# Turning tiles by way of DRAM instead of block by block, HGRN keys on TensorE, and a longer rest between narrow visits

## The chip, the core and the metric

The kernel runs on one core of a Trainium2 chip. The metric is the device time of one execution in microseconds (us). Engines are named as in the profile: PE is TensorE (matmuls; PEld is its weight load), DVE is VectorE, ACT is ScalarE, POOL is GpSimd, and SP is SyncE, whose queue issues nearly all DMAs.

## What is computed

One layer of a hybrid encoder on a sequence of 512 frames with 2048 features, in float32. One input projection feeds 16 RWKV-7 heads of 64 channels and 8 HGRN2 heads of 128 channels. Their gated outputs are concatenated, projected back, added to the input and normalized:

```python
proj = einsum('btd,dc->btc', x, w_in)
rw, hg = token_shift(proj[..., :RWKV_COLS]), proj[..., RWKV_COLS:]
# RWKV-7, per head: state S (64 x 64), one step a frame
S = S * w_t + (S @ -kk_t) (kk_t * a_t)^T + v_t k_t^T ;  o_t = S @ r_t
o = group_norm(o) * gn_w + gn_b + sum(r * k * r_k) * v ;  o_rwkv = o * silu(z)
# HGRN2, per head: gated linear recurrence, evaluated in chunks
o = chunkwise(silu(q), log_f, k, i) ;  o_hgrn = rms_norm(o) * g_norm_w * silu(z)
y = layer_norm(ALPHA * x + concat(o_rwkv, o_hgrn) @ w_out)
```

## The kernel before

The two projections are the bulk of the work. A float32 product is made from three float32r matmuls (high by high, high by low, low by high), so both operands are split into a high and a low part, on ScalarE and VectorE. Weights come in tiles `wr` of 512 KB, of which two are in flight; the split parts are `wh` and `wl`. These matmuls, issued at line 457, are called "main". The sequence `_order()` fixes which columns of the input projection are made when: eight RWKV pairs (two heads of 64 to a tile of 128 channels) and eight HGRN heads, in four groups of two pairs and two heads. The output projection follows, in four column blocks of 512; it takes its 16 k-tiles in the order `korder`, with pairs and heads 6 and 7 last.

Everything else (the recurrences, gates and norms) is put between the main matmuls by a planner, `Plan`, which runs while the program is written. It keeps a clock for each engine and SP, the time when each tile will be ready, and the time when it will be free, all from written-out costs. Side work lies in queues of Python generators. A generator yields operations, or tests that must hold before it goes on (`room(...)`: buffers are free; `has(...)`: another generator has delivered; `landed(...)`: PE would find the tiles ready by the planner's clock). After each main matmul `pump()` takes what can go next from every queue. The order that comes out is fixed in the program; on the chip the engines wait for each other by semaphores.

PE work has three modes: `main`, `whole` (128 x 128 stationary, float32) and `narrow` (a part of the array: 64 x 128, 128 x 32, 32 x 32 and so on). `Plan.worth` lets no narrow operation start in another mode until `REST` has gone by since the last narrow one ended (`self.rest = end + self.REST`, line 132).

The parts that the change touches:

- `send` (line 308) issues a DMA on SP's queue and moves the planner's SP clock.
- `turned` (line 397) transposes a tile without PE: VectorE transposes every 32 x 32 block in place (`dtr`), and DMAs from SBUF to SBUF then move each block to its place, one DMA for each block row and block column: 16 for `bk` and for the keys of a head, 8 for v.
- `rwkv_prep` (line 628) turns `bk` (beta and k, 128 x 1024) and v, the latter into the lower half of `z`, tile name `zz`, 128 x 8 x 128. `from_v` (751), `outputs` (772) and `rwkv_scan` (836) use `z` as the moving operand, chunk by chunk of 64 frames.
- `rwkv_finish` (901) ends a pair: group norm, four transposes on PE (line 925) into a PSUM tile, and scale, bias, `bv` and gate on VectorE.
- `hgrn_out` (1061) ends a head. It turns three blocks of keys, by `turned` for heads 0 to 5 and on PE for heads 6 and 7 (line 1075); makes the states and the output; norms it; and turns the output with four transposes on PE (line 1109).
- `put_gated` writes the gated tiles of pairs 0 to 5 and heads 0 to 5 to DRAM (`spill`); they are read back for the output projection.

Of the kernel before, what the change touches and what calls it, by code (L numbers as in the profile page):

```python
# [15 lines left out]
P = 128  # L16
# [7 lines left out]
NCH = T // C  # L24
# [38 lines left out]
class Plan:  # L63
# [178 lines left out]
def mixer_kernel(ctx, tc, head, x_r, w_all, par, up, ln_wb, consts, hmask, out):  # L242
# [41 lines left out]
    def drop(*tiles):  # L284
        for t in tiles:
            name = t.tensor.name
            plan.slots[tags.pop(name)].append((plan.used.get(name, plan.count), plan.busy[name][0]))

    def room(**need):

        return lambda: all(plan.free(tag, n) for tag, n in need.items())
# [13 lines left out]

        return test

    def send(o, i, cost=0.44):

        nc.sync.dma_start(o, i)  # L310
        plan.clock["sp"] = max(plan.clock["sp"], plan.clock["pe"]) + cost


    def size(ap):
# [55 lines left out]
    def dtr(o, i):  # L370
        return dve_op([i], o, lambda: dve.transpose(o, i), per=0.0019)
# [208 lines left out]
    def chunks(t):  # L580
        return t.rearrange("p (c s) -> p c s", s=C)
# [42 lines left out]
            ups.append(upw)  # L624

    hc = [slice(64 * h, 64 * h + 64) for h in range(2)]

    def rwkv_prep(S, p):
        if p == 0:
# [111 lines left out]
        S["bv"] = r  # L741

        yield room(zz=1)
        z = take("zz", [P, NCH, P])
        yield room(ksq=1)
        tmp = take("ksq")
        yield from turned(z, chunks(v), chunks(tmp), rows=2, base=64)
        drop(v, tmp)
        S["zz"] = z

    def from_v(SS, sc):

        yield lambda: all("zz" in S for S in SS)
        zs = [S["zz"] for S in SS]
        yield room(main=2, mix=1)
        yield landed(*zs, sc)
        pss = [take("main") for _ in SS]
        for half, (z, ps) in enumerate(zip(zs, pss)):
            for c in range(NCH):
                for h in range(2):  # L760
                    yield mm(ps[hc[h], c * C : c * C + C], sc[64:128, 0, half * 16 + 2 * c + h],
                             z[64:128, c, hc[h]])

        def keep():
            for z, ps in zip(zs, pss):
                for h in range(2):
                    yield copy(z[0:64, :, hc[h]], chunks(ps[hc[h]]))
                drop(ps)

        return keep  # L770

    def outputs(SS, sc):

        yield room(mix=2)
        pss = [take("mix") for _ in SS]
        for half, (S, po) in enumerate(zip(SS, pss)):
            z = S["zz"]
            yield lambda z=z: by_now(z)
            for c in range(0, NCH, 2):
                for h in range(2):  # L780
                    for e in range(2):
                        yield mm(po[hc[e], c // 2 * P + 64 * h : c // 2 * P + 64 * h + 64],
                                 sc[:, 1, half * 16 + 2 * (c + e) + h], z[:, c + e, hc[h]])
# [52 lines left out]
    def rwkv_scan(SS, sc):  # L836

        pcs, ars, bks, zzs, os = ([S[n] for S in SS] for n in ("pc", "ar", "bk", "zz", "o"))
        yield room(bd=4, rt=2)
        bdss = [[take("bd", [P, P]) for _ in range(2)] for _ in SS]
        rts = [take("rt", [P, P]) for _ in SS]

        def block(ps, h):
            return ps[hc[h], h * 64 : h * 64 + 64]

        for rt, bds, o in zip(rts, bdss, os):
            yield memset(rt[64:128], 0.0)  # L850
            for t in bds:
                yield memset(t, 0.0)
            yield memset(o[0:64, 0], 0.0)
        olds = [None] * 2
        for c in range(NCH):
            more = c < NCH - 1
            zs = [zz[:, c] for zz in zzs]
            news = [bds[c % 2] for bds in bdss]
            pxs = []
            if c > 0:  # L860
                yield landed(*olds)
                yield room(mix=2)
                for ar, old in zip(ars, olds):
                    pxs.append(take("mix"))
                    yield mm(pxs[-1][:, :P], ar[:, c], old)
                for rt, px, z in zip(rts, pxs, zs):
                    yield stt(rt[0:64], px[0:64, :P], -1.0, z[0:64], ALU.mult, ALU.subtract)
                if more:
                    for new, old, pc in zip(news, olds, pcs):
                        yield act(new, old, AF.Copy, scale=pc[:, c : c + 1])  # L870
            else:
                for rt, z in zip(rts, zs):
                    yield copy(rt[0:64], z[0:64], scale=-1.0)
            yield landed(*rts)
            yield room(mix=2)
            psas = [take("mix") for _ in SS]
            for half, (psa, rt) in enumerate(zip(psas, rts)):
                i = half * 16 + 2 * c
                yield mm(psa[:, :P], sc[:, 0, i : i + 2].rearrange("p h t -> p (h t)"), rt)
            for psa, z in zip(psas, zs):  # L880
                for h in range(2):
                    yield copy(z[0:64, hc[h]], block(psa, h))
                drop(psa)
            for px, o in zip(pxs, os):
                yield copy(o[64 * (c % 2) : 64 * (c % 2) + 64, c // 2], px[64:128, :P])
                drop(px)
            if more:
                yield landed(*zzs)
                yield room(mix=2)
                pds = [take("mix") for _ in SS]  # L890
                for pd, bk, z in zip(pds, bks, zs):
                    yield mm(pd[:, :P], bk[:, c], z)
                for pd, new, pc in zip(pds, news, pcs):
                    for h in range(2):
                        yield stt(new[hc[h], hc[h]], block(pd, h), pc[hc[h], c : c + 1],
                                  new[hc[h], hc[h]], ALU.mult, ALU.add)
                    drop(pd)
                olds = news
        drop(*ars, *bks, *pcs, *rts, *bdss[0], *bdss[1])

    def rwkv_finish(S, p):
# [16 lines left out]
        yield room(g=1, ksq=1)  # L918
        g = take("g")
        sz = take("ksq")  # L920
        z = S["z"]
        yield landed(o_all)
        po = take("mix")
        for j in range(4):
            yield tr(po[:, j * P : j * P + P], o_all[:, j])
        yield act(sz, z, AF.Tanh, scale=0.5)
        yield stt(g, po, hcol(HGW, p), S["bv"], ALU.mult, ALU.add)
        drop(po)
# [132 lines left out]
    def hgrn_out(S, h, q, k, dt_, dg, tot, tots):  # L1061
# [1 line left out]
        yield room(g=1)  # L1063
        g = take("g")
        kt, state = tiles(g)[:, 0:3], tiles(k)[:, 0:3]
        if h < 6:
            yield room(ksq=1)
            tmp = take("ksq")
            yield from turned(kt, tiles(k)[:, 0:3], tiles(tmp)[:, 0:3])
            drop(tmp)  # L1070
        else:
            yield landed(k)
            ps = take("mix")
            for t in range(3):
                yield tr(ps[:, t * P : t * P + P], k[:, t * P : t * P + P])
            yield copy(kt, tiles(ps)[:, 0:3])
            drop(ps)
        yield has(S, "i")
        yield room(rs=1)
        i_all = S["i"]  # L1080
# [25 lines left out]
        yield landed(o2)  # L1106
        pn = take("mix")
        for j in range(4):
            yield tr(pn[:, j * P : j * P + P], o2[:, j * P : j * P + P])
        yield has(S, "g")  # L1110
        yield stt(g, pn, hcol(HHW, h), S["g"], ALU.mult, ALU.mult)
        drop(S["g"], pn, o2)
        put_gated(8 + h, g)

    def silu2(ps, put):
# [561 lines left out]
```

## Time and profile before

| | |
|---|---|
| median of three runs | 1049.99 us (1049.23 to 1050.55) |
| the profiled execution | 1049.55 us |
| its span, first to last instruction | 1047.8 us |
| PE busy | 1039.1 us (99%), 7324 matmul records |
| DVE, ACT, POOL busy | 756.7, 437.9, 39.0 us |
| granted TensorE clock | 1.000 |
| DMA, main queue | 97824 packets, 114.57 MB |

In the profile, a row of the groups reads: line, engine, operation, output tile <- input tiles, shape, count | total busy time, mean of one in ns | idle time of the engine before them and what ended it. Buffer numbers are left out of tile names, so `q<-q` is any tile of the `q4` buffers from any other. A timeline row reads: start and duration in us, engine, line, operation, shape, count. A waits row reads: who <- for whom: total us, times, longest. The line of a helper stands for all who call it: 329 is every float32 matmul (`mm`), 333 every transpose on PE (`tr`), 310 every DMA (`send`), 371 every transpose on VectorE (`dtr`).

### The profile page before, as it was taken

Reading aid. Unit: us, or ns where it says so; the run is one execution under the profiler, and the core shown is the slowest. Engines: PE = TensorE matmul, PEld = TensorE weight load, DVE = VectorE, ACT = ScalarE, POOL = GpSimd, SP = SyncE. Lnnn points to the kernel's source line nnn. Section 1 sums busy time; section 2 is a strip of 40 time slices with the busy share of each in tenths; the row PEclk is TensorE's granted clock in tenths of the full one; section 3 lists DMA queues with packets and bytes.
Section 4 is the critical chain, followed back from the end, with each engine's and each line's share of the span. In section 5 each row is a group of like instructions: output and inputs, shape, how many; then the busy total and the mean of one; then the engine's idle time right before and its main releaser. Section 6 shows DMA issues by size and latency. Waiting matters only on the chain.

```text
span 1047.8 us, 18965 instructions
## 1 busy us (share of the span) xinstructions
PE 1039.1 (99%) x7324; PEld 864.3 (82%) x7324; DVE 756.7 (72%) x1649; ACT 437.9 (42%) x871; POOL 39.0 (4%) x81
## 2 busy tenths in 40 slices
PE   9999999999999999999999999999999999999997
PEld 8888888888888888887888888888888888888885
DVE  7474898767768987578689866686898878625556
ACT  6444433545344345353443354534434454223321
POOL 0000000000100000001000000010000001000000
PEclk9999999999999999999999999999999999999999
DMA  8135343222253532233534222225243244445613
GB/s 333 51 104 124 96 105 102 65 90 79 84 134 94 127 102 66 70 96 89 137 92 124 82 70 80 84 82 134 83 129 88 72 161 173 140 131 159 204 60 131
DMA packets 98058, 115.98 MB, mean 111 GB/s; under 512 B 67120, under 2 KB 68912, under 8 KB 97840
## 3 DMA queue, kind: packets, MB, share of 16 engines
q1 hardware_dynamic: 97824, 114.57, 37.5%
q8 instruction: 58, 0.95, 0.4%
q14 instruction: 32, 0.26, 0.1%
q10 hardware_dynamic: 144, 0.20, 0.1%
HBM read 99.92 MB, written 7.34 MB: 102 GB/s over the span
## 4 chain that ended last, share of the span: by engine, by line
PE 98%; DVE 1%; DMA 0%; issue 0%; SPq 0%; DVEq 0%
PE main L457 74%; PE mix L329 11%; PE mix L457 8%; PE main L1202 3%; PE main L329 2%; PE mix L333 1%; PE mix L1152 0%; DMA g<-ksq 0%; DVE inv L361 0%; DVE inv L352 0%; SPq L310 0%; DVE zz L394 0%; DVE stats L1559 0%; DVEq L1673 0%; DVE t L394 0%
## 5 line engine op out<-in xcount | busy, mean ns | idle before, releaser
L457 PE MATMUL main<-xh,wl 128*128 128x512 f32 x864 | 341.8, 396 | 0.0
L457 PE MATMUL main<-xh,wh 128*128 128x512 f32 x864 | 341.0, 395 | 0.0
L457 PE MATMUL main<-xl,wh 128*128 128x512 f32 x864 | 340.2, 394 | 0.0
L342 ACT ACTIVATE wh<-wr 128x512 fp32r<-128x512 f32 x299 | 187.0, 627 | 245.5 <-PE main L457 187.0
L352 DVE TENSOR_TENSOR wl<-wr,wh 128x512 fp32r<-128x512 f32 x299 | 203.2, 681 | 65.4 <-ACT wh L342 64.0
L457 PEld LDWEIGHTS main<-xl,wh 128*128 128x128 f32 x864 | 162.4, 188 | 33.2
L457 PEld LDWEIGHTS main<-xh,wh 128*128 128x128 f32 x864 | 162.5, 188 | 32.5
L457 PEld LDWEIGHTS main<-xh,wl 128*128 128x128 f32 x864 | 162.4, 188 | 32.6
L457 PE MATMUL main<-wh,xh 128*128 128x512 f32 (+1 forms) x262 | 102.2, 390 | 0.0
L457 PE MATMUL main<-wl,xh 128*128 128x512 f32 (+1 forms) x262 | 102.1, 390 | 0.0
L457 PE MATMUL main<-wh,xl 128*128 128x512 f32 (+1 forms) x262 | 102.0, 389 | 0.0
L457 PEld LDWEIGHTS main<-wh,xl 128*128 128x128 f32 x262 | 49.2, 188 | 9.8
L457 PEld LDWEIGHTS main<-wh,xh 128*128 128x128 f32 x262 | 49.2, 188 | 9.9
L457 PEld LDWEIGHTS main<-wl,xh 128*128 128x128 f32 x262 | 49.3, 188 | 9.5
L343 ACT ACTIVATE t<-main,om 128x512 f32<-128x512 f32 x33 | 22.3, 687 | 50.8 <-PE main L457 40.8
L361 DVE SCALAR_TENSOR_TENSOR t<-main,pr,t 128x511 f32<-128x511 f32 x33 | 24.3, 745 | 23.8 <-ACT t L343 23.5
L352 DVE TENSOR_TENSOR inv<-inv,inv 64x30 f32<-64x30 f32 (+14 forms) x120 | 38.6, 321 | 2.7
L352 DVE TENSOR_TENSOR inv<-inv 64x30 f32<-64x30 f32 (+14 forms) x120 | 38.5, 321 | 2.7
L361 DVE SCALAR_TENSOR_TENSOR bd<-mix,pc,bd 64x64 f32<-64x64 f32 x112 | 31.7, 283 | 11.0 <-PE mix L329 8.8
L352 DVE TENSOR_TENSOR t<-t,tot 128x256 f32<-128x256 f32 x96 | 37.2, 416 | 1.6 <-PE mix L329 1.3
L343 ACT ACTIVATE t<-main 128x512 f32<-128x512 f32 x32 | 18.7, 596 | 46.5 <-PE main L457 46.5
L384 POOL TENSOR_TENSOR rs<-rs,mhalf 128x4 f32<-128x4 f32 x8 | 10.8, 1346 | 496.9 <-DVE rs L358 496.9
(223 smaller groups left out, 1328.6 us busy)
## 6 DMA issues: line engine op xcount, KB each, us to landing
wr<-w_all SPq DMA_DIRECT2D x156, 512.0 KB, 3.6
q<-head SPq DMA_DIRECT2D x15, 448.0 KB, 5.5
q<-q SPq DMA_DIRECT2D x128, 32.0 KB, 2.6
g<-x_r SPq DMA_DIRECT2D x16, 256.0 KB, 3.8
spill<-g SPq DMA_DIRECT2D x12, 256.0 KB, 3.9
out<-q SPq DMA_DIRECT2D x12, 256.0 KB, 2.4
t<-spill SPq DMA_DIRECT2D x10, 256.0 KB, 4.1
zz<-ksq SPq DMA_DIRECT2D x64, 32.0 KB, 3.1
```

The lines of the kernel that those rows point to most:

```text
L329: return Op([("pe", cost, lambda: pe.matmul(o, l, r, start=start, stop=stop, **kw))], [l, r], [o], mode="narrow" if narrow else "main" if ...
L333: return Op([("pe", 0.11, lambda: pe.transpose(o, i, ident))], [i], [o])
L342: return "act", cost, lambda: sc_e.activation(o, i, f, scale=scale)
L343: return "act", cost, lambda: sc_e.activation(o, i, f, scale=scale, bias=bias)
L352: return dve_op([a, b], o, lambda: dve.tensor_tensor(o, a, b, f), base=0.16 if o.shape[0] < P and size(o) == C and o.tensor.name in tags e ...
L361: return dve_op([a, b], o, lambda: dve.scalar_tensor_tensor(o, a, s, b, f1, f2), per=0.00113, base=0.085 if o.shape[0] == P else 0.25 if s ...
L384: lambda: pool.tensor_tensor(o, i, mhalf[:, : size(o)], ALU.pow))], [i], [o])
L457: pe.matmul(ps, l, r, start=first and i == 0, stop=last and i == 2)
L1202: pe.matmul(pss[a], *ops, start=k == 0 and low == of == 0, stop=k == KT - 1 and low == 1)
```

## The change

`REST` goes from 1.5 to 2.5 us. `turned` now goes through DRAM: VectorE transposes the 32 x 32 blocks, one DMA writes the tile to a DRAM tile `far`, and one DMA for each 32 rows (four, or two for v) reads it back in its turned order. All blocks of one row then lie together, so the layout of what comes back is blocks of 32 columns, chunk by chunk. `z` keeps that layout ([128, 4, 8, 32] instead of [128, 8, 128]) and its users index it so; `bk` is copied to the old layout once more, on ScalarE or VectorE. Pairs 0 to 5 and heads 0 to 5 turn their ends through `turned` instead of on PE. The keys of heads 0 to 5 are transposed on PE, as those of 6 and 7 were. `from_v`, `outputs` and `rwkv_scan` do the same matmuls and copies on the new layout; of them the diff shows one line each of two. Where it says `else:`, the four transposes and the product of before follow.

```diff
-    REST = 1.5
+    REST = 2.5
...
-    def turned(dst, src, tmp, rows=4, base=0):
-        name = dst.tensor.name
-        yield dtr(tmp, src)
+    def turned(dst, src, tmp, base=0):
+        c = src.shape[1]
+        n = src.shape[2] // 32
+        yield dtr(tmp, src.rearrange("p c (b f) -> p b c f", f=32))
         yield lambda: by_now(tmp)
-        for a in range(4):
-            for b in range(rows):
-                yield lambda: plan.clock["sp"] <= plan.clock["pe"] + 0.2
-                o = base + 32 * b
-                send(dst[o : o + 32, :, 32 * a : 32 * a + 32],
-                     tmp[32 * a : 32 * a + 32, :, 32 * b : 32 * b + 32], 0.65)
-        plan.ready[name] = plan.busy[tmp.tensor.name] = (plan.clock["sp"] + 2.6, "dma")
+        far = dpool.tile([4, 32, n, c * 32], F32, tag=nm("far"), name=nm("far"))
+        yield lambda: plan.clock["sp"] <= plan.clock["pe"]
+        send(far.rearrange("a p b r -> (a p) b r"), tmp.rearrange("p b c f -> p b (c f)"))
+        at = plan.clock["sp"] + 3.7
+        plan.busy[tmp.tensor.name] = (at, "dma")
+        yield lambda: plan.clock["pe"] >= at
+        for b in range(n):
+            yield lambda: plan.clock["sp"] <= plan.clock["pe"]
+            o = base + 32 * b
+            send(dst[o : o + 32].rearrange("p a c f -> p a (c f)"), far[:, :, b].rearrange("a p r -> p a r"))
+        plan.ready[dst.tensor.name] = plan.busy[dst.tensor.name] = (plan.clock["sp"] + 3.5, "dma")
...
@@ rwkv_prep
-        yield from turned(bk, bk, tmp)
-        drop(tmp)
+        flat = bk.rearrange("p c t -> p (c t)")
+        yield from turned(blocks(flat, NCH), bk, blocks(tmp.rearrange("p c t -> p (c t)"), NCH))
+        yield copy(tmp.rearrange("p c (a f) -> p a c f", f=32), blocks(flat, NCH))
+        drop(bk)
+        S["bk"] = tmp
...
-        z = take("zz", [P, NCH, P])
+        z = take("zz", [P, 4, NCH, 32])
...
-        yield from turned(z, chunks(v), chunks(tmp), rows=2, base=64)
+        yield from turned(z, chunks(v), blocks(tmp, NCH), base=64)
@@ from_v, rwkv_scan
-                             z[64:128, c, hc[h]])
+                             z[64:128, hb[h], c])
...
-            zs = [zz[:, c] for zz in zzs]
+            zs = [zz[:, :, c] for zz in zzs]
...
@@ rwkv_finish
+        if p < 6:
+            yield from turned(blocks(S["ot"], 4), o_all, blocks(g, 4))
...
+        if p < 6:
+            yield act(in_blocks(g), blocks(S["ot"], 4).rearrange("p a c f -> p c a f"), AF.Identity,
+                      scale=hcol(HGW, p), bias=hcol(HGB, p))
+            yield act(sz, z, AF.Tanh, scale=0.5)
+            yield tt(g, g, S["bv"], ALU.add)
+        else:
+...
         yield stt(z, sz, 1.0, z, ALU.add, ALU.mult)
-        yield stt(g, g, hcol(HGB, p), z, ALU.add, ALU.mult)
+        if p < 6:
+            yield tt(g, g, z)
+        else:
+            yield stt(g, g, hcol(HGB, p), z, ALU.add, ALU.mult)
...
@@ hgrn_out
-        if h < 6:
-            yield room(ksq=1)
-            tmp = take("ksq")
-            yield from turned(kt, tiles(k)[:, 0:3], tiles(tmp)[:, 0:3])
-            drop(tmp)
-        else:
+        yield landed(k)
+        ps = take("mix")
+        for t in range(3):
+            yield tr(ps[:, t * P : t * P + P], k[:, t * P : t * P + P])
+        yield copy(kt, tiles(ps)[:, 0:3])
...
+        if h < 6:
+            yield from turned(blocks(o2, 4), tiles(o2), blocks(g, 4))
+            yield has(S, "g")
+            yield act(in_blocks(g), blocks(o2, 4).rearrange("p a c f -> p c a f"), AF.Copy, scale=hcol(HHW, h))
+            yield tt(g, g, S["g"])
+            drop(S["g"], o2)
+        else:
+...
```

More of the change, by code (lines that the diff above doesn't have):

```diff
@@ L306, in landed, with send @@
         return test
-    def send(o, i, cost=0.44):
+    def send(o, i):
         nc.sync.dma_start(o, i)
-        plan.clock["sp"] = max(plan.clock["sp"], plan.clock["pe"]) + cost
+        plan.clock["sp"] = max(plan.clock["sp"], plan.clock["pe"]) + 0.44
     def size(ap):
@@ L395, in copy, with in_blocks, blocks @@
         return Op([act_way(o, i, AF.Copy, scale), ("dve", 0.075 + size(o) * 0.00105 + moved(o, i), f)], [i], [o])
-    def turned(dst, src, tmp, rows=4, base=0):
-        name = dst.tensor.name
-        yield dtr(tmp, src)
+    def turned(dst, src, tmp, base=0):
+        c = src.shape[1]
+        n = src.shape[2] // 32
+        yield dtr(tmp, src.rearrange("p c (b f) -> p b c f", f=32))
         yield lambda: by_now(tmp)
-        for a in range(4):
-            for b in range(rows):
-                yield lambda: plan.clock["sp"] <= plan.clock["pe"] + 0.2
-                o = base + 32 * b
-                send(dst[o : o + 32, :, 32 * a : 32 * a + 32],
-                     tmp[32 * a : 32 * a + 32, :, 32 * b : 32 * b + 32], 0.65)
-        plan.ready[name] = plan.busy[tmp.tensor.name] = (plan.clock["sp"] + 2.6, "dma")
+        far = dpool.tile([4, 32, n, c * 32], F32, tag=nm("far"), name=nm("far"))
[9 more added lines that the diff above has]
+        plan.ready[dst.tensor.name] = plan.busy[dst.tensor.name] = (plan.clock["sp"] + 3.5, "dma")
+    def in_blocks(t):
+        return t.rearrange("p (c a f) -> p c a f", a=4, f=32)
+    def blocks(t, c):
+        return t.rearrange("p (a c f) -> p a c f", c=c, f=32)
     splits = plan.queue()
@@ L626, in mixer_kernel @@
     hc = [slice(64 * h, 64 * h + 64) for h in range(2)]
+    hb = [slice(2 * h, 2 * h + 2) for h in range(2)]
     def rwkv_prep(S, p):
@@ L766, in keep @@
                 for h in range(2):
-                    yield copy(z[0:64, :, hc[h]], chunks(ps[hc[h]]))
+                    yield copy(z[0:64, hb[h]], ps[hc[h]].rearrange("p (c a f) -> p a c f", c=NCH, f=32))
                 drop(ps)
@@ L782, in outputs @@
                         yield mm(po[hc[e], c // 2 * P + 64 * h : c // 2 * P + 64 * h + 64],
-                                 sc[:, 1, half * 16 + 2 * (c + e) + h], z[:, c + e, hc[h]])
+                                 sc[:, 1, half * 16 + 2 * (c + e) + h], z[:, hb[h], c + e])
         for S, po in zip(SS, pss):
@@ L847, in block, with by32 @@
             return ps[hc[h], h * 64 : h * 64 + 64]
+        def by32(t):
+            return t.rearrange("p (a f) -> p a f", f=32)
         for rt, bds, o in zip(rts, bdss, os):
@@ L866, in rwkv_scan @@
                 for rt, px, z in zip(rts, pxs, zs):
-                    yield stt(rt[0:64], px[0:64, :P], -1.0, z[0:64], ALU.mult, ALU.subtract)
+                    yield stt(by32(rt[0:64]), by32(px[0:64, :P]), -1.0, z[0:64], ALU.mult, ALU.subtract)
                 if more:
@@ L872, in rwkv_scan @@
                 for rt, z in zip(rts, zs):
-                    yield copy(rt[0:64], z[0:64], scale=-1.0)
+                    yield copy(by32(rt[0:64]), z[0:64], scale=-1.0)
             yield landed(*rts)
@@ L881, in rwkv_scan @@
                 for h in range(2):
-                    yield copy(z[0:64, hc[h]], block(psa, h))
+                    yield copy(z[0:64, hb[h]], by32(block(psa, h)))
                 drop(psa)
@@ L917, in rwkv_finish @@
         yield has(S, "z", "bv")
-        yield room(g=1, ksq=1)
+        yield room(g=1)
         g = take("g")
+        if p < 6:
+            yield from turned(blocks(S["ot"], 4), o_all, blocks(g, 4))
+        yield room(ksq=1)
         sz = take("ksq")
         z = S["z"]
[L922 to L928, printed above, removed]
+        if p < 6:
[4 more added lines that the diff above has]
+        else:
+            yield landed(o_all)
+            po = take("mix")
+            for j in range(4):
+                yield tr(po[:, j * P : j * P + P], o_all[:, j])
+            yield act(sz, z, AF.Tanh, scale=0.5)
+            yield stt(g, po, hcol(HGW, p), S["bv"], ALU.mult, ALU.add)
+            drop(po)
         yield stt(z, sz, 1.0, z, ALU.add, ALU.mult)
-        yield stt(g, g, hcol(HGB, p), z, ALU.add, ALU.mult)
+        if p < 6:
+            yield tt(g, g, z)
+        else:
+            yield stt(g, g, hcol(HGB, p), z, ALU.add, ALU.mult)
         drop(z, S["bv"], S["ot"], sz)
@@ L1065, in hgrn_out @@
         kt, state = tiles(g)[:, 0:3], tiles(k)[:, 0:3]
-        if h < 6:
-            yield room(ksq=1)
-            tmp = take("ksq")
-            yield from turned(kt, tiles(k)[:, 0:3], tiles(tmp)[:, 0:3])
-            drop(tmp)
-        else:
[L1072 to L1077, printed above, removed]
+        yield landed(k)
[3 more added lines that the diff above has]
+        yield copy(kt, tiles(ps)[:, 0:3])
+        drop(ps)
         yield has(S, "i")
@@ L1105, in hgrn_out @@
         S["used"]()
[L1106 to L1112, printed above, removed]
+        if h < 6:
[5 more added lines that the diff above has]
+        else:
+            yield landed(o2)
+            pn = take("mix")
+            for j in range(4):
+                yield tr(pn[:, j * P : j * P + P], o2[:, j * P : j * P + P])
+            yield has(S, "g")
+            yield stt(g, pn, hcol(HHW, h), S["g"], ALU.mult, ALU.mult)
+            drop(S["g"], pn, o2)
         put_gated(8 + h, g)
```

## The prediction, made before the change was run

> **What bounds the kernel now.** I read the head of the page first, then the chain that ended last, then what TensorE waited for.
>
> ```profile
> span 1047.8 us, 18965 instructions
> PE 1039.1 (99%) x7324; PEld 864.3 (82%) x7324; DVE 756.7 (72%) x1649; ACT 437.9 (42%) x871; POOL 39.0 (4%) x81
> DVE  7474898767768987578689866686898878625556
> PE 98%; DVE 1%; DMA 0%; issue 0%; SPq 0%; DVEq 0%
> ```
>
> TensorE is 98% of the chain. VectorE comes second at 72%, with slices at 8 and 9 tenths, but holds 1% of the chain. So almost the whole time is the sum of what TensorE is given to do; work put on other engines costs nothing until TensorE has to wait for it. These are two of the three waits that the profile lists for it:
>
> ```profile
> PE mix L329 <- ACT ksq L1419: 1.5, 1, 1.5
> PE mix L329 <- DMA g<-ksq: 1.2, 1, 1.2
> ```
>
> The second is the HGRN keys coming late from the block-by-block DMA turn, and this change takes that turn away. The first is in the tail, which stays.
>
> **Transposes on TensorE.** Row 333 of the kernel is the transpose; its price must be read from spacing, not duration. A visit of four, with main steps around it:
>
> ```profile
> L333 PE MATMUL mix<-cst,t 128*128 128x128 f32 x70 | 10.4, 272 | 0.0
> 892.72 0.39 PE L457 MATMUL main<-wh,xl 128*128 128x512 f32 x1
> ...
> 895.90 0.39 PE L457 MATMUL main<-wl,xh 128*128 128x512 f32 x1
> 896.13 0.60 PE L333 MATMUL mix<-cst,t 128*128 128x128 f32 x4
> 896.48 0.48 PE L457 MATMUL main<-wh,xl 128*128 128x512 f32 x1
> 896.80 0.39 PE L457 MATMUL main<-wh,xh 128*128 128x512 f32 x1
> ```
>
> From 892.72 to 895.90 are 14 main steps: 0.227 us each. From 895.90 to 896.80 there are two main steps (0.454) and the visit: 0.90 - 0.454 = 0.446 us for four transposes, 0.112 each. The 272 ns are the duration of one, most of which lies under its neighbours.
> Of the 70, the code has 32 at the RWKV ends, 32 at the HGRN ends, and 6 for the keys of heads 6 and 7. The change removes 4 x 6 + 4 x 6 = 48 in 12 visits: -12 x 0.446 = -5.35 us. It adds 3 x 6 = 18 for the keys of heads 0 to 5: +18 x 0.112 = +2.0 us. Net -3.3 us.
> The Trainium skill speaks against the half of this that leaves TensorE: "VectorE: DVE Perf Modes", section "Rules for kernel authors", says to transpose 128x128 on TensorE where a PSUM result will do, since VectorE turns only 32x32 blocks. The trace agrees on the blocks and shows the other side of the price: TensorE is the engine with no room.
>
> **The wait for the keys.** 1.2 us by the row above; keys now come from PSUM by a copy on ScalarE or VectorE. Between zero saved (the new copy comes as late) and 1.2, I take all of it, -1.2 us: the planner tests that tile as before, but its due time now rests on engine times instead of a transfer under load.
>
> **REST from 1.5 to 2.5 us.** It keeps TensorE from entering another narrow visit so soon. The closest pair that I found:
>
> ```profile
> 804.88 0.39 PE L457 MATMUL main<-xh,wh 128*128 128x512 f32 x1
> 805.20 0.75 PE L329 MATMUL mix<-big,inv 32*32 32x32 f32 x64
> 805.88 0.50 PE L457 MATMUL main<-xl,wh 128*128 128x512 f32 x1
> 806.22 0.40 PE L457 MATMUL main<-xh,wl 128*128 128x512 f32 x1
> ...
> 807.46 0.89 PE L329 MATMUL mix<-q,t 128*32 128x48 f32 x64
> ```
>
> Going in takes 0.32 us from start to start instead of 0.227, coming out 0.34: 0.2 us for a visit's two turns, saved if it is merged with the next. The code has nine narrow stretches to a group of two pairs and two heads, 36 in all over 1048 us, so most lie far apart; I count on one merge, -0.2 us, with 0 (none) and -0.6 (three) as ends. "TensorEngine Tiling (Array Packing)" of the Trainium skill, section "Tiling Modes", says that a change of tiling mode drains the array; the 0.2 us are what that costs here.
>
> **z in runs of 32.** The moving operand of the matmuls on z is now two or four runs of 32 columns. No such row exists; the nearest are the HGRN merges, which stream runs of 2 and 4 in their second stage (first visit below, group 0) and of 8 and 16 in their fourth (second visit, group 1):
>
> ```profile
> 175.53 0.39 PE L457 MATMUL main<-wh,xl 128*128 128x512 f32 x1
> ...
> 177.05 0.50 PE L457 MATMUL main<-wh,xh 128*128 128x512 f32 x1
> ```
>
> ```profile
> 409.96 0.39 PE L457 MATMUL main<-xh,wl 128*128 128x512 f32 x1
> ...
> 411.48 0.50 PE L457 MATMUL main<-xh,wh 128*128 128x512 f32 x1
> ```
>
> Both take 1.52 us for the same 128 instructions, so the length of a run does not show: 0, with less than 0.1 us either way over the few hundred matmuls on z.
>
> **The transfers.** These are replaced, with what SP took to issue one:
>
> ```profile
> q<-q SPq DMA_DIRECT2D x128, 32.0 KB, 2.6
> zz<-ksq SPq DMA_DIRECT2D x64, 32.0 KB, 3.1
> L310 SPq DMA_DIRECT2D g<-ksq x96: 585/597/1242, 202.5 to 666.1; - x96
> L310 SPq DMA_DIRECT2D t<-spill x10: 365/423/432, 836.4 to 877.1; - x10
> L310 SPq DMA_DIRECT2D spill<-g x12: 326/378/600, 231.6 to 757.9; - x12
> DMA to landing us min/median/max: 2.0/3.9/5.0
> wr<-w_all SPq DMA_DIRECT2D x156, 512.0 KB, 3.6
> ```
>
> 128 + 64 + 96 = 288 issues go, some 0.6 us each (that of the keys' row): 172 us of SP. What comes is one write and four or two reads for each turn: 8 x 5 (bk) + 8 x 3 (z) + 12 x 5 (ends) = 124 issues, 47 to 74 us by 0.38 and 0.6. SP gains 100 us and none of it is on the chain.
> Latency: a turn of bk was 16 x 0.65 + 2.6 = 13.0 us in the plan's own numbers, and becomes 0.44 + 3.7 + 4 x 0.44 + 3.5 = 9.4 and a copy; z goes from 7.8 to 8.5. The ends gain 9.4 us that they did not have. They lead only to a spill to DRAM, of which the last is issued at 757.9 us, and the first tile is read back at 836.4: cover of 78 us. Meanwhile an RWKV end holds three `t` tiles 9 us longer; were they lacking, evacuations would start late.
> What is new is that the reads wait at the head of SP's queue until the write has landed. The plan gives the write 4.14 us from its issue; the spills, also from SBUF to DRAM, land in 2.0 to 5.0, median 3.9 (the line under their row). Behind a late one stand the weight loads: up to 0.9 us, 28 times. What a late weight load costs is bounded by this row:
>
> ```profile
> ACT t L342 <- DMA wr<-w_all: 15.8, 8, 2.9
> ```
>
> ScalarE waited eight times for weights, once 2.9 us, and TensorE's list of waits has none for them. So 0.9 us is covered; I take 0. With no cover it would be 28 x 0.9 = 25 us.
>
> **VectorE and ScalarE.**
>
> ```profile
> L371 DVE STREAM_TRANSPOSE ksq<-t x14: 567/696/704, 89.9 to 782.6; 128x512 f32<-128x512 f32 x8, 128x384 f32<-128x384 f32 x6
> L371 DVE STREAM_TRANSPOSE inv<-big x8: 2000/2012/2044, 125.2 to 752.9; 32x1024 f32<-32x1024 f32 x8
> L361 DVE SCALAR_TENSOR_TENSOR g<-mix,half,t 128x512 f32<-128x512 f32 x16 | 11.9, 746 | 6.2 <-PE mix L333 6.0
> L352 DVE TENSOR_TENSOR wl<-wr,wh 128x512 fp32r<-128x512 f32 x299 | 203.2, 681 | 65.4 <-ACT wh L342 64.0
> L342 ACT ACTIVATE wh<-wr 128x512 fp32r<-128x512 f32 x299 | 187.0, 627 | 245.5 <-PE main L457 187.0
> ```
>
> VectorE loses 6 key transposes (0.57) and 18 scalar_tensor_tensor (0.75): -16.9 us. It gains 12 transposes of 512 columns (0.70, or 1.0 at the 2.0 ns a column of the strided row) and 18 products (0.68): 20.7 to 24.3. The eight copies of bk (1024 columns, up to 1.3) and six of keys (0.5) go to whichever engine is free: up to 13.4 more. So VectorE is 4 to 21 us busier of 291 idle, ScalarE 8 to 20 of 610. Nothing of this is on the chain, unless it delays the last group. There the cover is thin:
>
> ```profile
> 898.21 0.69 DVE L352 TENSOR_TENSOR xl<-g,xh 128x512 fp32r<-128x512 f32 x1
> 906.51 43.52 PE mix L457 x192
> ```
>
> The last HGRN head's gated tile is whole at 898.9; the second column block begins at 906.51, and each k-tile of the first takes 12 x 0.227 = 2.7 us, so the tile is needed at 906.51 - 2 x 2.7 = 901.1. Cover 2.2 us. Pairs and heads 6 and 7 keep their transposes, but bk, z and REST touch them. Lateness past 2.2 us is paid in full; I take 0, and up to 3 for the range.
>
> **Sum.** -3.3 - 1.2 - 0.2 = -4.7 us. The profiled execution took 1049.55 us, of which 1047.8 are the span: 1044.8 after. It stands 0.4 below the median of the runs, 1049.99; from that, 1045.2 us, which I predict.
>
> **Rivals.**
> 1. Slower, through SP's queue. Reads parked behind their own write hold back weights at 28 turns. It turns the result to slower when it costs TensorE more than (4.7 + 2.1) / 28 = 0.24 us a turn; if half of the 0.9 us showed at each, 13 us, the time is 1058. "DMA: Bandwidth & Descriptors" of the Trainium skill, section "Two DMAs through the same engine are not ordered", says the wait cannot be avoided: a read of written bytes must wait for the write's semaphore. Against it: weights 2.9 us late cost nothing. Chance 0.09.
> 2. No change, 1049. The last group comes 2 to 5 us past its cover, or a few transfers land after their due time as the keys did once, and the saving goes there. For it: the 2.2 us of cover, and a written order that shifts throughout. Against: TensorE now waits directly on only one kind of turned tile, z, ahead of the inversion's products. Chance 0.17.
> 3. The change does more: each transpose is worth its whole duration, 30 x 0.272 = 8.2 us, and the time is 1040.4. "TensorE: Matmul & The Clock Gate" of the Trainium skill, section "Part 4: PE-mode transpose", gives about 275 ns for one in a kernel; the duration here agrees, the spacing in the rows says 112. Chance 0.04.
>
> **How the numbers follow.** The forecast has 0.70, and its own range is 1043 to 1047.5: the ends of the wait (1.2), the merges (-0.4, +0.2) and up to 1 us of new waits. Within 0.2% (2.1 us) is about what a measurement of this kernel can tell from no change. Faster by more than that: forecast and rival 3, 0.74; same 0.16 and slower 0.10, rival 2 falling mostly within. The range of 8 in 10 takes in most of rival 2: 1042.5 to 1050.
>
> **What would show it.** Transposes on row 333's successor fall from 70 to 40 with the same spacing; no wait of TensorE for `g<-ksq`; narrow visits fewer by one or so; TensorE still 98% of the chain. Wrong would be: TensorE waiting for `wh` or `wl` after SP stood at a read of `far` (rival 1), for `xh` or `xl` near 900 us or for `zz` (rival 2), or matmuls on z spaced wider than before.

## Result: slower by 0.65%, and the profile after

The changed kernel takes 1056.93 us, median of four runs (1055.32 to 1057.77), against 1049.87 us of the kernel before beside it: a ratio of 1.0065, 95% interval 1.0054 to 1.0077. The prediction was 1045.2 us in a range of 1042.5 to 1050: wrong, in size and in sign. The profiled execution took 1057.77 us, 1056.0 of them its span; before it was 1047.8, so 8.2 us have to be found. (One run of experiment 3, at 1151.62 us, and one of the kernel before beside experiments 1 to 4 were disturbed, and all figures here leave them out.)

The engines' busy times, and the chain that ended last:

```profile
PE 1040.6 (99%) x7294; PEld 863.1 (82%) x7294; DVE 756.9 (72%) x1654; ACT 455.1 (43%) x898; POOL 37.9 (4%) x81
PE 92%; DVE 3%; DMA 2%; ACT 2%; issue 1%; SPq 0%; DVEq 0%; ACTq 0%
```

TensorE's share of the chain fell from 98% to 92%. Its busy time should have fallen by the transposes and rose by 1.5 us instead. So there are two questions: for what it waits, and what made it slower while busy. The whole list of its waits:

```profile
PE mix L329 <- issue: 3.3, 2, 2.0
PE mix L329 <- DVE ksq L352: 2.6, 4, 1.4
PE mix L329 <- ACT ksq L1452: 1.5, 1, 1.5
PE mix L1185 <- DVE inv L1183: 1.1, 1, 1.1
PE mix L329 <- ACT ksq L342: 0.8, 1, 0.8
PE mix L329 <- DVE t L352: 0.4, 1, 0.4
PE mix L329 <- DVE bd L361: 0.4, 1, 0.4
PE mix L329 <- DVE zz L394: 0.4, 1, 0.4
```

The rows for L1452 and L1185 belong to the tail and the start and were there before. The keys' `g<-ksq` is gone. New are two stops with releaser "issue", five waits for `ksq`, and three small ones. A row counts only the idle time after the modelled end of the matmul before, so each is 0.1 to 0.4 us shorter than what is lost from start to start.

**The two stops.** TensorE's timeline around the first, and the row that ends the second:

```profile
179.23 0.39 PE L470 MATMUL main<-wl,xh 128*128 128x512 f32 x1
179.54 0.71 PE L329 MATMUL mix<-t 128*32 128x16 f32 x62
...
180.79 2.08 PE L329 MATMUL main<-zz,big 64*64 64x64 f32 x64
182.81 0.85 PE L329 MATMUL mix<-inv,big 32*32 32x32 f32 x43
184.99 0.52 PE L329 MATMUL mix<-inv,big 32*32 32x32 f32 x21 [1.33 <-issue]
...
615.39 0.34 PE L329 MATMUL mix<-big,inv 32*32 32x32 f32 x18 [2.00 <-issue]
```

From 179.54 on, three narrow stretches of 128, 64 and 64 matmul records follow each other with no main step between. In the middle of the last, after 235 records, TensorE does nothing, and no semaphore is named for it (the row's "issue"). The second stop comes after 174 records of a merged stretch of 192 that begins at 611.59. The matmuls behind a stop are slow, as the windows show (the window and its length, PE, PEld, DVE, ACT, POOL with counts, granted clock, DMA share, GB/s):

```profile
183.60:185.00 1.40, 0.07 (x5) 0.01 (x3) 0.82 (x2) 0.00 (x0) 0.00 (x0) 1.00 0.00 0
185.40:189.50 4.10, 4.10 (x17) 3.19 (x12) 2.90 (x9) 2.75 (x7) 0.00 (x0) 0.62 0.02 4
616.40:619.80 3.40, 3.40 (x9) 2.66 (x9) 1.36 (x3) 1.95 (x6) 0.00 (x0) 0.51 0.06 7
```

The granted clock goes to half for some 3.4 us; 15 main steps there take 0.427 us instead of 0.227. The stops lose 1.56 and 2.19 us from start to start, the half clock 15 x 0.2 and a few steps in between, about 3.3: 7.0 us together. The slow steps are the surplus in PE's busy time.

The traces show what TensorE stood for: its instructions. A view of the DMA queues for 611 to 616 us has one packet in all, of the queue that the profile calls "instruction" (a row reads: packets, MB, share of 16 engines):

```profile
q8 instruction: 1, 0.02, 1.3%
```

It is 16 KB, and ran from 613.08 to 614.11; TensorE went on at 615.39, 1.28 us after its end. At the first stop such a packet ran from 182.71 to 183.67, and TensorE went on 1.32 us after its end. Over the whole run this queue moves 57 packets, one for some 256 of TensorE's 14588 records (a matmul and a weight load each count one). So a packet lasts for 128 matmuls: some 29 us of main steps, but in the first stretch the 128 matmuls from 179.54 took 1.25 us, while 2.3 us pass from the start of a packet until TensorE goes on.

**The late turn of bk.** The five waits for `ksq` make four standstills of one kind, at 348.67, 568.86, 723.11 and 773.33. SP, ScalarE and TensorE around the first of these:

```profile
336.25 0.43 SPq L310 DMA_DIRECT2D far<-q  x1
341.49 1.74 SPq L310 DMA_DIRECT2D q<-far  x4
348.18 1.06 ACT L342 ACTIVATE q<-q 128x1024 f32<-128x1024 f32 x1 [3.67 <-DMA q<-far]
349.15 0.61 ACT L342 ACTIVATE ksq<-t 128x512 fp32r<-128x512 f32 x1
348.67 0.39 PE L470 MATMUL main<-xh,wh 128*128 128x512 f32 x1
349.81 0.49 PE L329 MATMUL mix<-ksq,ones_r 128*128 128x512 f32 x1 [0.76 <-ACT ksq L342]
```

The write is issued at 336.25, the four reads go from 341.49 on, and ScalarE, whose next instruction is the copy of `bk`, stands 3.67 us for them. Behind the copy in its queue lies the split of r, which has nothing to do with `bk`; TensorE wants that split, and its next matmul starts 1.14 us after the last main step instead of 0.23. The rows below are from the DMA issues (KB each, median us from issue to landing) and from ScalarE's waits:

```profile
far<-q SPq DMA_DIRECT2D x8, 512.0 KB, 5.2
q<-far SPq DMA_DIRECT2D x32, 128.0 KB, 4.5
```

```profile
ACT q L342 <- DMA q<-far: 15.2, 5, 3.7
```

The plan gave the write 4.14 us from its issue and the reads 3.94. The four standstills cost TensorE 4.6 us from start to start. The smaller waits (251.0, 458.2, 671.7) cost 1.6.

So 7.0 + 4.6 + 1.6 = 13.2 us were lost. On the other side the transposes are down as counted (70 before):

```profile
L333 PE MATMUL mix<-cst,t 128*128 128x128 f32 x40 | 6.2, 272 | 0.0
```

With the wait for the keys gone and 33 narrow visits now 30, the prediction's own prices give 3.3 + 1.2 + 0.6 = 5.1 us saved: 13.2 - 5.1 = 8.1 of the 8.2 us. The 5.1 is worked out, not measured by itself.

### The profile page after: what moved, and what is told of

Same layout as the page of the kernel before. It is cut to its first block, busy times and chain, and to the rows that moved or that the text cites. A ratio compares the mean times of both kernels' runs of the same rounds, so it can differ in the third digit from the quotient of the medians.

```text
span 1056.0 us, 18747 instructions
## 1 busy us (share of the span) xinstructions
PE 1040.6 (99%) x7294; PEld 863.1 (82%) x7294; DVE 756.9 (72%) x1654; ACT 455.1 (43%) x898; POOL 37.9 (4%) x81
## 4 chain that ended last, share of the span: by engine, by line
PE 92%; DVE 3%; DMA 2%; ACT 2%; issue 1%; SPq 0%; DVEq 0%; ACTq 0%
PE main L470 68%; PE mix L329 10%; PE mix L470 8%; PE main L1235 3%; PE main L329 2%; DMA q<-far 1%; DVE wl L352 1%; DVE inv L352 1%; DMA far<-q 0%; ACT L343 0%; PE mix L1185 0%; PE mix L333 0%; DVE inv L361 0%; DVE ksq L352 0%; ACT wh L342 0%
## 5 line engine op out<-in xcount | busy, mean ns | idle before, releaser
L342 ACT ACTIVATE zz<-mix 64x64 f32<-64x64 f32 x73 | 15.9, 218 | 43.4 <-PE mix L329 42.6
```

What stands on the lines that cost most here:

```text
L342: return "act", cost, lambda: sc_e.activation(o, i, f, scale=scale)
```

## Experiments

**1. REST.** The changed kernel with `REST = 1.5`: did the longer rest merge the stretches?

> The changed kernel with REST back at 1.5 us, everything else as changed. In the changed kernel's trace TensorE stops twice inside a long narrow stretch with nothing to wait for (at 183.4 us for 1.33 us in a stretch of 256 matmul records, at 613.2 us for 2.0 us in one of 192), and after each stop some eight main matmuls run at 0.427 us instead of 0.227: about 3.3 + 3.0 = 6.3 us. Theory A: the longer rest gathers narrow work into those stretches; then 1.5 us parts them and the time is about 1050.5 us. Theory B: the rest has nothing to do with it (in the written order the two long stretches are there at 1.5 us as well); they come about because the side work of one group reaches TensorE at the same moment; then the time stays at 1056 to 1058 us, with two stops of that kind in the trace.

Measured: 1054.74 us (1053.74 to 1055.32), ratio 1.0046, 1.003 to 1.0061. Both merged stretches and both stops stay, at 183.9 and 613.7:

```profile
PE mix L329 <- issue: 3.6, 2, 2.3
```

`REST` merged neither, and is worth about 2 us at most: the intervals overlap. The narrow visits are 30 here too, so the fall from 33 was not its doing either.

**2. A cap on narrow stretches.** The changed kernel, and in `Plan.worth`, with `self.row` counting the narrow operations of the running visit (64 of them are 128 matmul records in the trace):

```diff
+        if op.mode == "narrow" == self.mode and self.row >= 64:
+            return False
```

> The changed kernel with one more rule in the planner: after 64 narrow matmuls in one visit it must go back to main work first, so no stretch has over 128 matmul records. If the two stops come from the length of the stretch (TensorE uses up its instructions faster than new ones are fetched), both stops and the matmuls at 0.427 us go: 1056.9 - 3.3 - 3.0 + 0.6 (three more turns of 0.2) = about 1051 us, and no wait by 'issue' on TensorE. If they come from something else at these places (a tile, a bank), stops of 1 to 2 us stay and the time is 1056 to 1058 us.

Measured: 1058.25 us (1057.33 to 1063.48), 1.0097, 1.0066 to 1.0128. No stretch is longer than 128 records, and the stops in them are nearly gone (one of 0.4 us left), but the order has moved and the copy of `bk` strikes elsewhere. ScalarE and VectorE, then the windows:

```profile
303.72 1.06 ACT L345 ACTIVATE q<-q 128x1024 f32<-128x1024 f32 x1 [7.13 <-DMA t<-far]
305.33 0.69 DVE L355 TENSOR_TENSOR wl<-wr,wh 128x512 fp32r<-128x512 f32 x1 [7.87 <-ACT wh L345]
```

```profile
303.60:305.40 1.80, 0.05 (x1) 0.05 (x1) 0.07 (x1) 1.68 (x3) 0.00 (x0) 1.00 0.00 0
306.00:309.20 3.20, 3.20 (x8) 2.48 (x8) 3.18 (x7) 2.08 (x5) 0.00 (x0) 0.51 0.56 164
```

The copy holds ScalarE for 7.13 us (the row names the DMA that came last by the profile; the copy itself reads `q<-far`), the split of the weights stands behind it, and TensorE stops for 1.8 us between main steps. The half clock follows here too, with no narrow stretch ahead: here it comes behind a stop alone. (In experiment 8 it comes behind narrow work alone.)

**3. Due times as measured.** The changed kernel, told how long its transfers take:

```diff
-        at = plan.clock["sp"] + 3.7
+        at = plan.clock["sp"] + (5.2 if c * n == 32 else 4.4)
...
-        plan.ready[...] = plan.busy[...] = (plan.clock["sp"] + 3.5, "dma")
+        plan.ready[...] = plan.busy[...] = (plan.clock["sp"] + 5.0, "dma")
```

> The changed kernel with later due times in the turn by way of DRAM: the write 5.2 us after its issue for 512 KB and 4.4 for 256 KB instead of 3.7, the reads 5.0 instead of 3.5. Measured in the changed kernel: the 512 KB write landed after 5.2 us (median), the last read of bk up to 2.4 us past its due time; ScalarE then stood 2.3 to 3.7 us at the copy of bk in four of eight pairs, the split of r behind it came late, and TensorE waited for it 0.8 to 1.8 us each time, 4.7 us in all. Theory: with honest due times the copy is put where the data are there, ScalarE waits for q<-far under 3 us in all, TensorE's waits for ksq go, and the time falls by 4 to 6 us to about 1052 us (the stops inside narrow stretches stay, unless the order shifts). Rival: the wait is not in the due time but in the transfers' load, which gets no smaller; then the waits move with the due times and the time stays within 1.5 us of 1056.9.

Measured: 1056.57 us (1055.63 to 1058.81, three runs), 1.0068, 1.005 to 1.0086. The waits for `ksq` go from 3.4 us to 0.3 and ScalarE's at the copy from 15.2 to 8.9, but the stops stay and new small waits come:

```profile
PE mix L329 <- issue: 3.2, 2, 1.8
...
PE mix L333 <- DVE t L352: 0.9, 1, 0.9
...
PE mix L329 <- DVE ksq L352: 0.3, 1, 0.3
```

The late transfer is the cause of those waits. No time is won: TensorE now waits several times between 880 and 897 us, for the last group. I take that for work that the later due times push toward the end; no run isolates it.

**4. Both together.**

> Both rules of the two kernels before. If the stops in long narrow stretches and the late turns explain all that went wrong, what is left is the saving that was predicted: -3.3 us of transposes and -1.2 us of the old wait, so 1045 to 1047 us. If a third cause of some size is there, the time stays above 1049 us.

Measured: 1049.40 us, ten runs (1047.79 to 1050.30), 0.9993, 0.9984 to 1.0003: 7.5 us better than the changed kernel, where neither edit alone helped. In the traced execution (1048.67 us) no stop and no half clock is left, and one stall:

```profile
464.17 0.40 PE L473 MATMUL main<-xh,wl 128*128 128x512 f32 x1
466.22 0.71 PE L332 MATMUL mix<-rt,big 128*128 128x128 f32 x4 [1.66 <-DVE rt L364]
467.68 0.50 PE L473 MATMUL main<-xh,wh 128*128 128x512 f32 x1 [0.74 <-DVE t L364]
```

It costs 2.6 us from start to start. The span is 0.9 us below the kernel before, so without the stall it would be 3.5 us below: most of the 4.5 us priced for transposes and keys (the visits are 33 again, so no merge is saved). The stall fits `t` tiles held too long by an RWKV end, but I infer that from the order; no run here isolates it. Of the ten runs, the five at a granted clock of 1.000 took 1047.8 to 1049.1 us and the five at 0.998 took 1049.7 to 1050.3; what slows those was not traced.

**5. Keys alone.** The kernel before with the keys of heads 0 to 5 transposed on TensorE, by the lines of heads 6 and 7.

> The kernel before with one part of the change: the keys of heads 0 to 5 transposed on TensorE. By the prediction's prices: +2.0 us of transposes, -1.2 us of the wait for the old turn: 1050.7 us, and no new wait of TensorE. A rival is that any part that shifts the order brings waits of its own: then 1052 us or more, with waits that have nothing to do with keys.

Measured: 1051.30 us (1050.21 to 1052.56), 1.0013, 1.0003 to 1.0022. 18 more transposes against a wait of 1.2 us: a small loss, and no new wait.

**6. Ends alone.** The kernel before with only the ends of pairs and heads 0 to 5 by DRAM (`turned` as changed, for them alone).

> The kernel before with the ends of pairs and heads 0 to 5 by way of DRAM, with the change's due times, and nothing else. By the prediction's prices -5.35 us: 1044.5 us. If the ends also bring ScalarE's stands at the late reads (in the changed kernel it stood 16.6 us in seven places for t<-far), TensorE waits behind them 1 to 3 us in all and the time is 1046 to 1048 us.

Measured: 1075.23 us (1074.62 to 1077.22), 1.0243, 1.0226 to 1.026. Windows for the main matmuls alone:

```profile
433.00:445.00 12.00, 11.40 (x46) 7.86 (x44) 1.00 0.29 66
446.00:458.00 12.00, 0.00 (x0) 0.00 (x0) 0.80 0.07 22
```

For 12 us there was no main step at all, and once more at 861 to 873. With no main work to fill in, the waits of the scan show, and the stops come too:

```profile
PE mix L329 <- DVE bd L361: 5.9, 7, 1.7
PE mix L329 <- issue: 3.5, 2, 1.8
```

The planner found no main work that it could place. That the evacuations (the copies that take finished projection columns out of PSUM) had no free `t` tile, held 9 us longer by the ends on top of the old keys' turn, is my reading of the order, again not isolated.

**7. bk and v alone.** The kernel before with bk and v by DRAM, the copy of `bk` and the new layout of `z`; `REST`, keys and ends as before.

> The kernel before with beta, k and v by way of DRAM, the new layout of z and the copy of bk, and nothing else (REST 1.5, keys and ends as before). By the prediction 0: 1049.9 us. If the late turn of bk is what costs 4.7 us in the changed kernel, it is 1053 to 1055 us, with ScalarE standing at the copy of bk and TensorE waiting for ksq behind it; its written order also has two stretches of 256 narrow matmul records, so up to two stops without a releaser of 1.3 to 2 us each, and a few us at half clock, come on top: up to 1060 us.

Measured: 1056.65 us (1055.16 to 1058.47), 1.0069, 1.0054 to 1.0084: as large a loss as that of the whole change. The stops in merged stretches are there, at 183.3 and 608.35, and so is ScalarE at the copy:

```profile
PE main L329 <- issue: 1.5, 1, 1.5
...
PE mix L329 <- issue: 1.3, 1, 1.3
```

```profile
ACT q L342 <- DMA q<-far: 12.9, 4, 4.6
```

But TensorE waits only 0.2 us for `ksq` here. The loss is mostly the two stops (3.2 us from start to start) and half clock behind each, and not the late turn that I had expected to cost 3 to 5 us. A late copy costs TensorE only where something wanted soon stands behind it.

**8. Long stretches on purpose.** The kernel before, each set of 32 x 32 products of `quarters` written four times over (the extra three are wasted work): do stops come from length alone?

```diff
+            for _ in range(4):
                 for j in range(8):
                     for g in range(4):
                         yield mm(pq[32 * g : 32 * g + 32, j], *prod(8 * g + j))
```

> The kernel before, in which each of the inversion's two sets of 32 x 32 products is written four times over instead of once (the same products into the same place): nothing of the change is in it, and no tile comes later for it, but narrow stretches grow to 320 to 384 matmul records. The extra work is 24 sets of 64 records at 0.65 us: +15.6 us, 1065.5 us. If TensorE runs out of instructions in long narrow stretches, it stops with no releaser for 1 to 2 us in most stretches over 235 records, with half clock behind some of the stops: 1072 to 1085 us. If the stops of the changed kernel came from its late tiles, none is seen here and the time is 1065 to 1067 us.

Measured: 1101.74 us, one run, so no interval. The extra matmuls are some 15.6 us of it. Below are the waits by "issue", two windows as in the table of the two stops, and the timeline around the first stop.

```profile
PE mix L329 <- issue: 14.0, 10, 2.3
180.40:183.70 3.30, 3.30 (x179) 3.23 (x178) 2.24 (x5) 1.47 (x3) 0.00 (x0) 1.00 0.50 164
183.80:184.50 0.70, 0.70 (x54) 0.63 (x44) 0.70 (x4) 0.00 (x0) 0.00 (x0) 0.50 0.00 0
183.28 1.29 PE L329 MATMUL mix<-inv,big 32*32 32x32 f32 x75
185.80 1.48 PE L329 MATMUL mix<-inv,big 32*32 32x32 f32 x89 [1.23 <-issue]
```

There are ten stops, and 63 main steps at half clock. Nothing in this kernel goes by DRAM that did not before: length alone brings the stops; I had expected 1072 to 1085 us. The windows show something more. The clock is at half from 183.75 on, after 3.3 us of narrow work without a gap, and the first stop comes only behind that, at 184.57. So the half clock does not need a stop.

**9. What to keep.** The changed kernel with the cap, and `bk` turned the old way, in 16 block DMAs without a copy; due times as in the change.

> The changed kernel with the limit of 64 narrow matmuls to a visit, and with bk alone turned the old way, block by block from SBUF to SBUF and without a copy; v, the ends, the keys and REST as changed, due times as changed. With the limit alone (bk by way of DRAM) the time was 1058.25 us. Theory: bk's late turn and its copy, at which ScalarE stood, are the second cause; without them TensorE has no wait for ksq and no wait of over 1 us but those of the tail and the start, and the predicted saving of 4.7 us appears: 1045 to 1047 us. Rival: the ends' reads (t<-far) hold ScalarE as much as bk's did; then TensorE still waits 3 us or more in all and the time is 1049 us or above.

Measured: 1046.83 us (1046.12 to 1047.75), 0.9971, 0.996 to 0.9982, the best of all and faster than both kernels. Against experiment 2, which differs in the turn of `bk` alone, it is 11.4 us. The old turn without the cap was not run. Beyond start and tail TensorE waits only for

```profile
PE mix L332 <- DVE ksq L355: 0.8, 2, 0.5
PE main L489 <- DVE wl L355: 0.2, 1, 0.2
```

although ScalarE still stands 13.4 us for `t<-far` at the ends: there nothing queued behind it is wanted soon.

**10 and 11. Which ends pay.** The kernel before with keys on TensorE, the cap, `REST = 1.5`, and ends by DRAM: all twelve (first), then those of HGRN alone.

> The kernel before with keys on TensorE and the ends by way of DRAM, and the limit of 64; beta, k and v turned the old way, REST 1.5. By the prediction's prices -5.35 + 2.0 - 1.2 = -4.5 us: 1045.4 us. The ends alone, with the keys turned the old way, took 1075.2 us, with TensorE without main work at 445 to 478 us and 861 to 873 us: no `t` tile was free for the results of the projection, because the ends hold them longer. Theory: with keys on TensorE a head holds its tiles some 10 us less, which gives most of them back, so those stretches are gone or under 3 us in all: 1045 to 1048.5 us. Rival: the ends themselves are too long for 18 tiles; then the stretches stay and the time is over 1055 us.

> As the kernel before in this list, but only the HGRN ends of heads 0 to 5 go by way of DRAM; the RWKV ends, which hold three `t` tiles each while they wait, stay on TensorE. By the prices -2.7 + 2.0 - 1.2 = -1.9 us: 1048 us, with no stretch of TensorE without main work.

Measured: 1047.36 us (1046.81 to 1048.59), 0.9976, 0.9967 to 0.9985; and 1048.59 us (1048.29 to 1049.26), 0.9988, 0.9979 to 0.9997. By the medians the RWKV ends are worth 1.2 us more, though the intervals overlap. The gaps of experiment 6 are gone, but experiment 10 differs from it in the keys and in the cap, so which of the two ended them is not shown.

**12. The cap alone,** on the kernel before, as the control.

> The kernel before with the limit of 64 alone, as the control. It had one stretch of 192 narrow records (at 186 us) and no stop in it, so the limit only adds a turn of 0.2 us and shifts the order: 1050 us, within 1 us. If the limit itself is worth something, it would be 1048 us or less.

Measured: 1048.47 us (1048.05 to 1049.12), 0.9989, 0.998 to 0.9998. I had expected no change: the moved order happens to lose the keys' wait of 1.2 us. So of the 2.6 us of experiment 10, about 1.5 came by the cap or with it.

## Why the prediction was wrong, by its own steps

**The priced terms: right, one of them by luck.** Transposes went from 70 to 40, the keys' wait is gone, and 64 matmuls on z take 2.08 us on runs of 32 as they did before (at 180.79, and at 605.51 in the kernel before). Visits fell by three where one was counted on, but not by `REST`: experiment 1 has 30 as well. By their prices that is 5.1 us where the sum said 4.7; experiment 4, without the merges, is 3.5 us below the kernel before but for its stall, against 4.5. What failed is what the sum left out.

**"REST from 1.5 to 2.5 us": wrong in what a merge costs, and in who merges.** The step priced a merge as a gain of 0.2 us, with 0 and -0.6 as ends, and excluded a loss for no reason. The two merged stretches shown above hold both stops, which cost 7.0 us with the half clock behind them. And not `REST` merged them: they stay without it (experiment 1), and the turn of bk alone brings such stretches (7). The prediction's list of what is supplied to TensorE had operands and weights but not instructions. The trace of before holds a visit of 192 records, from 186.01 to 187.89 us, without a stop, so no row there priced it; its instruction packets start at 183.50 and 187.80, none of them inside the first 1.8 us of the visit. It should have been a term bounded on both sides.

That a stop is a wait for instructions rests on three things: no semaphore ends it, length alone makes it (8), and the packets lie where they must. The traces hold 21 stops of over 0.2 us with releaser "issue" (here, and in experiments 1, 2, 3, 6, 7 and 8). In each, a 16 KB packet of the instruction queue starts 2.2 to 2.8 us before TensorE goes on and ends 1.2 to 1.5 us before. What fills the time from its end to the next matmul, and just when the next packet is asked for, the profile does not tell. The Trainium skill, "Runtime: NRT & Kernel Launch", section "Instruction fetch mechanics", agrees on blocks of 16 KiB, and says that crossing one is "mostly hidden". In dense narrow stretches the traces differ: 0.4 to 2.3 us, in sight.

**"VectorE and ScalarE": the step that failed for the other 4.6 us.** It said that the copies of bk "go to whichever engine is free" and "Nothing of this is on the chain". It costed the copy by its duration (up to 1.3 us; 1.06 measured) and not by the wait in front of it, nor by what is queued behind it on an engine that works in order. A copy that waits 3.7 us for a DMA costs ScalarE 4.7, and r's split is behind it.

**"The transfers": right on SP, wrong on the latency.** SP never held back weights to TensorE's cost in the changed kernel: its waits name no `wh` or `wl`, so rival 1 is out, though its 1058 is close to the time measured. The turn was taken at the plan's 3.7 and 3.5; I had set a spill's 5.0 against that only for the weights behind, not for the data itself. Rival 2's "a few transfers land after their due time" was near this, but priced within the saving and on a direct wait of TensorE.

**The hold on `t` tiles** was named, and priced at nothing. It did not decide here. Experiment 6 suggests that with the old turn of keys it would have been worth some 25 us, but the cause of that gap is inferred. What also stays open is what decides whether half clock follows a stop.

## What to carry to other kernels

Price a step put on an engine that works in order by the wait ahead of it and by what stands behind it, not by its duration: a late transfer stops everything in that queue. When TensorE gets long runs of tiny matmuls, break them with large ones (here after 64 of the planner's operations, which are 128 records): by their busy time the runs cost nothing, but in the changed kernel they stopped after 174 and 235 records. When a change is made of parts, try the parts alone and in pairs: here one part alone lost as much as the whole, two mends helped only together, and the rest, with the cap, was worth 3 us, of which the cap alone gives 1.5.

## What the runs showed of the hardware that was not expected

In experiment 2 the clock went to half for about 3.4 us behind a stop of 1.8 us between main steps. "TensorE: Matmul & The Clock Gate" of the Trainium skill, section "Part 1: The HAM clock gate", names an idle window of some 3.4 us for that; the runs show it after less, and the length of the slow stretch agrees. In experiment 8 it came after 3.3 us of narrow matmuls with no idle time at all. Not every stop does it. In each trace the changes of the granted clock lie whole multiples of 3.413 us apart (186.38, 189.79, 616.46 and 619.87 in the changed kernel), so it may matter where a stop falls between two such times. The traces do not settle it: of two stretches of 3.4 us filled with narrow work and a stop of under 0.5 us, the one in experiment 1 (from 181.17) was followed by half clock, and the one in experiment 3 (from 180.31) was not.

TensorE's instructions come in packets of 16 KB for some 256 records (57 packets in the changed kernel), and a narrow stretch can use them up faster than they come: that is the reading of the 21 stops of 0.4 to 2.3 us. A 512 KB write to DRAM followed by four reads took 11.9 us from issue to use at 336.25, against 9.4 and a copy in the plan.
